# A two-block layer on one core: four products turned to tokens on partitions, seven accumulators in the first pass, and two paces of the scan

## The chip, the cores and the metric

One core of a Trainium2 chip runs the whole program. The metric is the time of one execution on the device in microseconds (us), smaller is better; the runs of before gave 2216.6, 2218.7 and 2218.76 us, median 2218.7 us.

## What is computed

Two blocks act one after the other on x, 256 tokens by 2048 features; the second (attention and a recurrent mix, then a gated feed-forward) is not touched. The first, cut to what matters:

```python
h = rmsnorm(x, norm_g)
proj = einsum('bld,dn->bln', h, w_in)
v, bg, cg, za, u, zb, ga, gb = split(proj, SPLITS)   # 2048 x4, 1024 x2, 2048 x2 columns
ya = bg * causal_depthwise_conv(cg * v, conv_w)
ya = einsum('blc,cd->bld', ya * silu(za), w_out_a)
yb = gelu(s5_scan(u, ...))                           # 64 groups, 64 complex states each
yb = yb * sigmoid(yb @ w_glu + b_glu)
yb = einsum('blc,cd->bld', yb * silu(zb), w_out_b)
m = sigmoid(ga) * ya + sigmoid(gb) * yb
return x + einsum('bld,de->ble', m, w_o)             # then rmsnorm with final_g
```

All of it is in 32-bit floats. To keep that precision on TensorE, each operand is split into a high part (rounded to fp32r) and a low part (the rest), and a product is the sum of high x high, low x high and high x low.

## The kernel before

**Weights.** All weights come in blocks of 128 x 1024 floats (512 KB), in the order in which the program wants them: `weights` makes the list from `W1` and `W2`, `sub` (line 241) hands out 128 columns of the present block. A block is loaded into `wf` by SyncE's queue, four ahead. ScalarE casts it to the high part `wh` (line 142 is every ScalarE operation), and VectorE subtracts to get the low part `wl` (line 132 is every two-operand operation on VectorE or GpSimd). Cast and split are recorded three blocks ahead of the use.

**Products.** `gemm` (line 255) makes 128 outputs for 256 tokens with the outputs on partitions: per 128 x 128 weight tile one matmul with `wh` stationary and the 512 columns of x's high and low part moving, and one with `wl` stationary and the 256 columns of the high part. This text calls the two a pair. The result lies in two halves of a PSUM bank, which are added when they are read: `take` (line 285) is a ScalarE copy, a VectorE add, and, where asked, a VectorE multiply with `R`, the reciprocal norm of each token. `v_in` (line 1392), in the second block, makes its product the other way around: x is stationary, 128 tokens at a time, and 512 weight columns move; three matmuls of 512 columns (high x high, high x low, low x high) per half of the tokens. Its result has tokens on partitions.

**Order of the work.** The program is written out in order for every engine; nothing is scheduled afterwards. `later` (line 156) starts a generator whose steps are recorded between the matmuls: each pair calls `tick` once, and a `yield n` lets n ticks pass (without a number, the task's default). `flush` records what is left at once. So a step's place among the matmuls is fixed, and each engine does its own list in order.

**First block.** `_block1` (line 792) loads and scales x (`X`), and runs `w_in`: a first pass over 12 of 16 rows of X with eight PSUM accumulators, one per tile of 128 columns of u, then the last four rows tile by tile (`u_out`). PSUM has eight banks, three named `acc` and five named `pb`. `squares` adds the squares of x on ScalarE and GpSimd, `first_norm` waits 96 ticks and has `rstd` (line 336) sum them with a matmul into `st`, and spread the result `R` with another into `al`. Then follow 16 rounds of v, cg, bg, za, each 16 pairs, which leave `Ya`. Then come w_out_a (to DRAM as `ya_out`), `w_in_g` (the columns of zb, ga, gb), w_glu, w_out_b with `merge_out`, and w_o with `x1_out`.

**The scan.** `s5` (line 621) runs as a task beside all this from the second row of X to the end of gb. `s5_prep` (line 421) makes its constants in steps of 8 ticks; `s5_base` (line 567) makes a table on GpSimd in steps of 1 to 3. Then come 32 steps of six yields of 8 ticks: two matmuls into `bu`, two VectorE products, two GpSimd sums, two VectorE scans (line 683), a GpSimd and a VectorE product, two GpSimd differences, and a table for the next step (ScalarE and GpSimd). Every fourth step sums its output with matmuls into `y` and starts `gelu`. `s5_stage` (line 554) brings the inputs by DMAs that GpSimd issues. At the end the rows of yb are split (`Yh`), which w_glu reads.

Of the kernel before, what the change touches and what calls it, by code (L numbers as in the profile page):

```python
# [10 lines left out]
F32 = mybir.dt.float32  # L11
F32R = mybir.dt.float32r
I32 = mybir.dt.int32
AF = mybir.ActivationFunctionType
# [72 lines left out]
class K:  # L87
# [74 lines left out]
    def _go(self, t):  # L162
        try:
            r = next(t[0])
            t[1] = t[3] if r is None else r
            return True
        except StopIteration:
            t[0] = None
            return False
# [136 lines left out]
    def hl(self, n, name="x"):  # L306

        c = [self.chunk(F32R, name) for _ in range((n + 3) // 4)]
        both = lambda k: self.flat(c[k // 4])[:, 512 * (k % 4):512 * (k % 4) + 512]
        return [(both(k)[:, 0:256], both(k)[:, 256:512], both(k)) for k in range(n)]  # L310

# [309 lines left out]
    def s5(self, U):  # L621

        nc, g = self.nc, self.nc.gpsimd
        for n in self.s5_prep():
            yield n or 8
        self.stg = self.flat(self.chunk(F32R, "stg")).rearrange("p (h i j t) -> p h i j t", h=2, i=2, j=2)
        stage = self.later(self.s5_stage(0), ev=False)
        cb = self.flat(self.cbd).rearrange("p (i k c) -> p i k c", i=2, k=32)
# [114 lines left out]
        yield  # L743
        self.tt(dst, z[:], sg[:], eng=self.nc.gpsimd)

    def ga_out(self, p, dst, ya):
        z, sg = self.tmp("z"), self.tmp("sg")
        yield from self.take(p, z[:], self.R[:])
        yield
        self.act(sg[:] if ya is not None else dst, z[:], AF.Sigmoid)  # L750
        if ya is not None:
            yield
            self.tt(dst, sg[:], ya[:], eng=self.nc.gpsimd)

    def glu_out(self, p, q, y, zb, dst):
        sg, t = self.tmp("sg"), self.tmp("ya")
        self.tt(t[:], y, zb, eng=self.nc.gpsimd)
# [8 lines left out]
        yield  # L766
        yield from self.hilo(t[:], dst)

    def merge_out(self, p, gb, ga, dst):
        t = self.tmp("ya")  # L770
        yield from self.take(p, t[:], gb)
        yield
        self.tt(t[:], t[:], ga, ALU.add, self.nc.gpsimd)
        yield
        yield from self.hilo(t[:], dst)

    def x1_out(self, p, n, x1, xin, dst):
        self.add(p, x1)
# [13 lines left out]
    def _block1(self):  # L792
        nc, g = self.nc, self.nc.gpsimd
        R, R2 = self.R, self.R2
        xin = [self.chunk(name="x") for _ in range(2)]
        X = self.hl(16, "X")

        def load(b):
            nc.sync.dma_start(out=xin[b // 4][:, 2 * (b % 4):2 * (b % 4) + 2], in_=self.i["x"][:, 2 * b:2 * b + 2])

        def scale(k):
            src = xin[k // 8][:, k % 8]
            g_ = self.vec("norm_g", k)
            self.act(X[k][0], src, scale=g_)
            self.stt(X[k][1], src, g_, X[k][0].bitcast(F32), ALU.mult, ALU.subtract)

        def squares():
            for k in range(16):
                sq = self.square(0, xin[k // 8][:, k % 8], first=k == 0)
                yield 2  # L810
                self.add_square(sq)
                yield 3
            self.squared = True

        for b in range(4):
# [12 lines left out]

        def first_norm():
            yield 96  # L830
            self.act(self.eps[:, 2:3], self.eps[:, 0:1], AF.Sqrt)
            yield 8
            yield from self.rstd(1, self.rt, R[:])
            self.tt(R2[:], R[:], R[:])

        self.setup2()
        norm = self.later(first_norm(), default=4)
        self.fg1 = self.const.tile([128, 16], F32, name="fg1")
        self.tt(self.fg1[:], self.vec("final_g"), self.vec("norm1_g"))
        U, uh = self.chunk(name="u"), [self.chunk(F32R, "uh") for _ in range(2)]  # L840
        self.cv = [self.const.tile([128, 258], F32, name=f"cv{i}") for i in range(2)]
        for c in self.cv:
            nc.vector.memset(c[:, 0:2], 0.0)
        ps = [self.pb("acc") if q in (0, 2, 4, 6, 7) else self.acc() for q in range(8)]
        self.s5u, self.s5b = ([self.dram.tile([128, 8, 256], F32, name=f"s5{n}{i}") for i in range(2)] for n in "ub")
        self.gelus, self.u_done, self.squared = 0, 0, False
        self.later(squares(), ev=False)
        for k in range(12):
            if k + 5 < 16:
                scale(k + 5)  # L850
            if k == 1:
                s5 = self.later(self.s5(U), ev=False, default=8)
            for p in ps:
                self.gemm(X[k:k + 1], p, k == 0, False)
        for q in range(8):
            p = self.gemm(X[12:16], ps[q], False, True)
            self.later(self.u_out(p, q, U[:, q], [c[:, q] for c in uh]))
        Ya = self.hl(16, "ya")
        for f in range(16):
            p = self.gemm(X)  # L860
            if f == 0:
                self.flush(norm)
            vs = self.tmp("vs", bufs=1)
# [10 lines left out]
        ya_out = self.dram.tile([128, 16, 256], F32, name="ya_out")  # L874
        for n in range(16):
            p = self.gemm(Ya)
            t = self.tmp("yo")
            self.take_now(p, t[:])
            nc.sync.dma_start(out=ya_out[:, n], in_=t[:])
        Ga, Zb = [self.chunk(name="ga") for _ in range(2)], self.chunk(name="zb")  # L880
        for q in range(8):
            p = self.gemm(X)
            self.later(self.silu_out(p, Zb[:, q]))
        for n in range(16):
            t = self.tmp("yo")
            nc.sync.dma_start(out=t[:], in_=ya_out[:, n])
            p = self.gemm(X)
            self.later(self.ga_out(p, Ga[n // 8][:, n % 8], t))
        Gb = [self.chunk(name="gb") for _ in range(2)]
        for n in range(16):  # L890
            p = self.gemm(X)
            self.later(self.ga_out(p, Gb[n // 8][:, n % 8], None))
# [12 lines left out]
        for n in range(16):  # L905
            p = self.gemm(Yg)
            self.later(self.merge_out(p, Gb[n // 8][:, n % 8], Ga[n // 8][:, n % 8], M[n]))
        xin = [self.chunk(name="x") for _ in range(2)]
        for k in range(0, 16, 8):
            nc.sync.dma_start(out=xin[k // 8][:], in_=self.i["x"][:, k:k + 8])  # L910
        self.x1 = self.dram.tile([128, 16, 256], F32, name="x1")
        self.flush()
        X2 = self.hl(16, "X")
        for n in range(16):
            p = self.gemm(M)
            self.later(self.x1_out(p, n, xin[n // 8][:, n % 8], xin, X2[n]))
            if n == 12:
                self.act(self.eps[:, 2:3], self.eps[:, 0:1], AF.Sqrt)
        self.flush()
        return X2  # L920

# [648 lines left out]


W2 = ("z_in", "v_in0", "v_in1", "qk_in", "v_in2", "w_out_at", "w_out_rw", "gate_up0", "down0", "gate_up1", "down1")
W1 = ("w_in", "w_out_a", "w_in_g", "w_glu", "w_out_b", "w_o")


def tiles(w, cols=128, kblk=None):
# [16 lines left out]
def layout(a):  # L1593
# [10 lines left out]
    u = r["w_in"][:16].reshape(8, 2, 128, 8, 128)  # L1604
    u = u.transpose(1, 3, 2, 0, 4).reshape(16, 128, 8, 128)
    r["w_in"][:12] = u[:12].reshape(12, 128, 1024)
    r["w_in"][12:16] = u[12:].reshape(4, 128, 4, 2, 128).transpose(2, 1, 3, 0, 4).reshape(4, 128, 1024)
    r["w_in_g"] = tiles(part(72, 40))
    for n in ("w_out_a", "w_glu", "w_out_b", "w_o"):
        r[n] = tiles(a[n][0])  # L1610
# [75 lines left out]
```

## Time and profile before

| | |
|---|---|
| median of three runs | 2218.7 us (2216.6 to 2218.76) |
| profiled execution | 2216.1 us, span of its instructions 2214.4 us |
| mean granted TensorE clock | 0.991 |
| first block | from 6.3 us (first matmul) to 944 us |

How to read the views: the page gives each engine's busy time and, in 40 slices of 55 us, its busy tenths. The table of waits says which engine stood idle before an instruction and what ended it. A row on a tile lists the instructions that read or write it, with shortest, median and longest duration and the first and last start. A row on a stretch gives each engine's busy time in it and the number of instructions. The timeline gives start, duration, engine, line, operation, and in brackets the idle time ahead of it and its releaser. Durations of matmuls are modelled ends; their starts are exact, so rates are read from starts.

### The profile page before, as it was taken

To read this page: it belongs to the slowest core of one execution; us is meant where nothing else is said; L and a number is where in the kernel's file an instruction comes from. 1 tells how busy PE (TensorE), PEld (TensorE's weight loads), DVE (VectorE), ACT (ScalarE), POOL (GpSimd) and SP (SyncE) were. 2 spreads that over 40 slices of the span, in tenths; PEclk is the share of its full clock that TensorE was granted. 3 is DMA by queue.
4 is the path that set the end of the run, shared out by engine and by line. 5 is a ranking of instruction groups with operands and counts; after the bars stand their busy time and mean duration, and the time that the engine had idled before them with its cause. 6 is when DMAs were issued, how large, how long until landed. Compare 5 with 4: busy or idle time off the path is not lost.

```text
span 2214.4 us, 37860 instructions
## 1 busy us (share of the span) xinstructions
PE 2151.8 (97%) x14500; PEld 1886.5 (85%) x14500; DVE 1655.3 (75%) x2396; ACT 1129.6 (51%) x1871; POOL 800.3 (36%) x930
## 2 busy tenths in 40 slices
PE   7899999999999999999989999999999999999997
PEld 6788888878888888899989888888888888888886
DVE  8889999987898678766896978976665555666554
ACT  5465555555555565544544544554444334444443
POOL 4768888866897012323330000421111001111111
PEclk9999999999999999999999999999999999999998
DMA  7586665667676657665646535566666666666653
GB/s 243 170 252 187 185 180 181 191 196 219 186 213 208 186 180 229 209 203 184 181 134 198 165 113 178 176 182 190 186 185 190 184 188 184 188 186 186 190 182 113
DMA packets 141842, 414.13 MB, mean 187 GB/s; under 512 B 27403, under 2 KB 46140, under 8 KB 140508
## 3 DMA queue, kind: packets, MB, share of 16 engines
q1 hardware_dynamic: 132540, 400.98, 59.3%
q0 software_dynamic: 8256, 8.40, 1.5%
q8 instruction: 114, 1.87, 0.3%
q10 hardware_dynamic: 864, 2.33, 0.3%
q14 instruction: 68, 0.56, 0.1%
HBM read 397.99 MB, written 15.75 MB: 187 GB/s over the span
## 4 chain that ended last, share of the span: by engine, by line
PE 75%; DVE 13%; DMA 4%; POOL 3%; issue 3%; ACT 1%; SPq 0%; DVEq 0%; ACTq 0%; POOLq 0%
PE acc L145 72%; DVE wl L132 5%; DMA wf<-z_in 2%; POOL s L132 1%; ACT wh L142 1%; PE y L145 1%; DMA wf<-w_in 1%; DVE gb L132 1%; DVE att L132 1%; DVE s L132 1%; DMA stg<-s5b 1%; DVE s L683 1%; DVE cv L132 0%; DVE ya L132 0%; POOL ab L132 0%
## 5 line engine op out<-in xcount | busy, mean ns | idle before, releaser
L145 PE MATMUL acc<-X,wh 128*128 128x512 f32 (+1 forms) x4576 | 1391.8, 366 | 6.3 <-ACT wh L142 6.3
L132 DVE TENSOR_TENSOR wl<-wf,wh 128x1024 fp32r<-128x1024 f32 (+1 forms) x711 | 937.8, 1322 | 306.3 <-ACT wh L142 302.1
L145 PE MATMUL acc<-X,wl 128*128 128x256 f32 x3888 | 1065.8, 283 | 14.6 <-DVE wl L132 14.5
L142 ACT ACTIVATE wh<-wf 128x1024 fp32r<-128x1024 f32 (+1 forms) x711 | 748.5, 1054 | 490.0 <-PE acc L145 339.3
L145 PEld LDWEIGHTS acc<-X,wh 128*128 128x128 f32 x4576 | 810.4, 190 | 140.9 <-ACT wh L142 6.3
L145 PEld LDWEIGHTS acc<-X,wl 128*128 128x128 f32 x3888 | 739.1, 190 | 42.1 <-DVE wl L132 22.8
L132 POOL TENSOR_TENSOR z<-z,R 128x256 f32<-128x256 f32 x44 | 58.9, 1338 | 523.4 <-ACT sg L142 523.4
L145 PE MATMUL acc<-s,wh 128*128 128x512 f32 (+1 forms) x726 | 246.8, 392 | 0.0
L132 POOL TENSOR_TENSOR s<-s 128x32 f32<-128x32 f32 (+4 forms) x272 | 223.7, 842 | 35.4 <-DVE s L132 19.1
L145 PE MATMUL acc<-s,wl 128*128 128x256 f32 x704 | 192.7, 281 | 0.0
L145 PEld LDWEIGHTS acc<-s,wh 128*128 128x128 f32 x726 | 133.0, 188 | 28.9
L132 POOL TENSOR_TENSOR sum<-sum,sq 128x256 f32<-128x256 f32 x74 | 71.4, 974 | 222.4 <-ACT sq L142 222.0
L145 PEld LDWEIGHTS acc<-s,wl 128*128 128x128 f32 x704 | 133.0, 189 | 3.2
L132 POOL TENSOR_TENSOR s<-s,s 128x256 f32<-128x256 f32 (+1 forms) x80 | 102.7, 1300 | 38.6 <-DVE s L132 24.4
L142 ACT ACTIVATE z<-acc 128x256 f32<-128x256 f32 x100 | 38.1, 381 | 117.2 <-PE acc L145 117.0
L145 PE MATMUL acc<-ya,wh 128*128 128x512 f32 x256 | 91.1, 403 | 0.1
L145 PE MATMUL acc<-m,wh 128*128 128x512 f32 x256 | 89.3, 398 | 0.0
L132 POOL TENSOR_TENSOR bv<-bv,gs 128x128 f32<-128x128 f32 x16 | 13.2, 832 | 205.4 <-DVE bv L139 205.4
L132 DVE TENSOR_TENSOR h<-acc,h 128x256 f32<-128x256 f32 x111 | 46.9, 422 | 43.0 <-PE acc L145 39.6
L142 ACT ACTIVATE s<-s,s 128x64 f32<-128x64 f32 (+2 forms) x192 | 69.4, 409 | 12.8 <-POOL s L132 11.6
L132 DVE TENSOR_TENSOR z<-acc,z 128x256 f32<-128x256 f32 x100 | 41.7, 417 | 45.2 <-ACT z L142 45.2
L145 PE MATMUL acc<-ya,wl 128*128 128x256 f32 x256 | 70.3, 284 | 4.0 <-ACT ya L142 3.1
(279 smaller groups left out, 2490.4 us busy)
## 6 DMA issues: line engine op xcount, KB each, us to landing
wf<-gate_up SPq DMA_DIRECT2D x176, 512.0 KB, 3.5
wf<-w_in SPq DMA_DIRECT2D x143, 512.0 KB, 4.4
wf<-down SPq DMA_DIRECT2D x88, 512.0 KB, 3.6
wf<-w_in_g SPq DMA_DIRECT2D x80, 512.0 KB, 3.6
wf<-z_in SPq DMA_DIRECT2D x54, 512.0 KB, 4.9
wf<-w_out_a SPq DMA_DIRECT2D x32, 512.0 KB, 4.3
wf<-w_o SPq DMA_DIRECT2D x32, 512.0 KB, 4.2
wf<-qk_in SPq DMA_DIRECT2D x32, 512.0 KB, 4.1
```

Source lines behind the costliest of these rows:

```text
L132: (eng or self.nc.vector).tensor_tensor(out=out, in0=a, in1=b, op=op)
L142: self.nc.scalar.activation(out=out, in_=a, func=f, **k)
L145: self.nc.tensor.matmul(out, l, r, start=start, stop=stop)
L683: nc.vector.tensor_tensor_scan(out=s[:, 256 * i:256 * i + 256], data0=r, data1=x[:, 256 * i:256 * i + 256], initial=0.0, op0=ALU.mult, op1 ...
```

## The change

1. **Tokens on partitions.** `by_token` replaces `gemm` for w_out_a, ga, gb and w_out_b, in the manner of `v_in`: for each 512 outputs two accumulators (one `acc`, one `pb`), one per half of the tokens, three matmuls of 512 columns each per row of x, and a tick for every 256 outputs. The four weight matrices are laid out in tiles of 512 columns for it. The results are read by one operation: w_out_a by a ScalarE copy, the gates by a ScalarE sigmoid whose scale is the token's reciprocal norm (`ga_out`), w_out_b by a VectorE multiply with the gate (`merge_out`). The sum of both branches is then turned back to features on partitions by TensorE transposes (`mt`), 32 in all, and split into `M`; the first w_o product starts on its first 12 rows before the last are made.
2. **Seven tiles of u.** The first pass has seven accumulators (three `acc`, four `pb`); the eighth tile is a product of 16 pairs behind the others. `first_norm` waits 62 ticks in place of 96, `squares` 4 per row in place of 5. The weights of u are laid out in the new order.
3. **Two paces.** A yield of the scan lasts 10 ticks up to the end of w_in (1152 pairs) and 7 afterwards, in place of 8; one of its setup 9 in place of 8.

```diff
     def _go(self, t):
         try:
             r = next(t[0])
-            t[1] = t[3] if r is None else r
+            t[1] = r if r is not None else t[3]() if callable(t[3]) else t[3]
...
     def s5(self, U):
         for n in self.s5_prep():
-            yield n or 8
+            yield n or 9
...
+    def by_token(self, xs, out):
+        n = len(xs)
+        for c in range(4):
+            ps = [self.acc(), self.pb("acc")]
+            for k in range(n):
+                wh, wl = self.sub(4)
+                xh, xl, _ = xs[k]
+                for t in range(2):
+                    ts_ = slice(128 * t, 128 * t + 128)
+                    self.mm(ps[t][:], xh[:, ts_], wh, k == 0, False)
+                    self.mm(ps[t][:], xh[:, ts_], wl, False, False)
+                    self.mm(ps[t][:], xl[:, ts_], wh, False, k == n - 1)
+                    if k == n - 1:
+                        out(c, t, ps[t])
+                    self.tick()
+                    self.tick()
+
+    def ga_out(self, p, t, dst, ya):
+        self.act(dst, p[:], AF.Sigmoid, scale=self.rt[:, t:t + 1])
+        if ya is not None:
+            yield 4
+            self.tt(dst, dst, ya[:], eng=self.nc.gpsimd)
+
+    def merge_out(self, p, c, t, ga, gb, M):
+        cs = slice(512 * c, 512 * c + 512)
+        self.tt(gb[t][:, cs], p[:], gb[t][:, cs])
+        yield 3
+        self.tt(ga[t][:, cs], ga[t][:, cs], gb[t][:, cs], ALU.add, self.nc.gpsimd)
+        if t == 0:
+            return
+        yield 6
+        for i in range(2):
+            n = 4 * c + 2 * i
+            q = self.pb("mt")
+            for j in range(4):
+                o = 128 * (n + j // 2)
+                self.nc.tensor.transpose(q[:, 128 * j:128 * j + 128], ga[j % 2][:, o:o + 128], self.ident[:])
+            v = M[n // 4][:, 512 * (n % 4):512 * (n % 4) + 1024].rearrange("p (k i t) -> p k i t", k=2, i=2)
+            yield from self.hilo(q[:].rearrange("p (k t) -> p k t", k=2), (v[:, 0], v[:, 1]))
...
                 self.add_square(sq)
-                yield 3
+                yield 2
...
         def first_norm():
-            yield 96
+            yield 62
...
-        ps = [self.pb("acc") if q in (0, 2, 4, 6, 7) else self.acc() for q in range(8)]
+        ps = [self.acc() if q in (1, 3, 5) else self.pb("acc") for q in range(7)]
...
-                s5 = self.later(self.s5(U), ev=False, default=8)
+                s5 = self.later(self.s5(U), ev=False, default=lambda: 10 if self.n_sub < 1152 else 7)
...
-            p = self.gemm(X[12:16], ps[q], False, True)
+            p = self.gemm(X[12:16], ps[q], False, True) if q < 7 else self.gemm(X, self.pb("acc"))
...
-        for n in range(16):
-            p = self.gemm(Ya)
-            t = self.tmp("yo")
-            self.take_now(p, t[:])
-            nc.sync.dma_start(out=ya_out[:, n], in_=t[:])
+        def wa_out(c, t, p):
+            y = self.tmp("yo", 512)
+            self.act(y[:], p[:])
+            nc.sync.dma_start(out=ya_out[:, t, 512 * c:512 * c + 512], in_=y[:])
+
+        self.by_token(Ya, wa_out)
...
-        for n in range(16):
-            p = self.gemm(Yg)
-            self.later(self.merge_out(p, Gb[n // 8][:, n % 8], Ga[n // 8][:, n % 8], M[n]))
+        mc = self.hl_chunks
+        self.by_token(Yg, lambda c, t, p: self.later(self.merge_out(p, c, t, Ga, Gb, mc)))
...
-            p = self.gemm(M)
+            if n == 0:
+                p = self.acc()
+                self.gemm(M[0:12], p, True, False)
+                self.flush()
+                X2 = self.hl(16, "X")
+                p = self.gemm(M[12:16], p, False, True)
+            else:
+                p = self.gemm(M)
```

Where instructions move, on TensorE. First, the sums of squares, matmul `st`, in the u stage (`acc` are the accumulators, X the rows of x). Before it stands behind the products of the second tile's last four rows:

```order
L145 MATMUL acc_167<-X_101,wl_501 128x256
L145 MATMUL acc_167<-X_101,wh_489 128x512
L145 MATMUL acc_167<-X_101,wl_501 128x256 x2
L145 MATMUL acc_167<-X_101,wh_489 128x512
L145 MATMUL st_604<-ones,sum_88 128x1 x2
L145 MATMUL acc_168<-X_101,wh_521 128x512
L145 MATMUL acc_168<-X_101,wl_531 128x256
```

Now it stands in the first pass, at the end of the tenth row:

```order
L145 MATMUL acc_171<-X_100,wl_374 128x256
L145 MATMUL acc_172<-X_100,wh_351 128x512
L145 MATMUL acc_172<-X_100,wl_374 128x256
L145 MATMUL st_476<-ones,sum_88 128x1 x2
L145 MATMUL acc_166<-X_100,wh_351 128x512
L145 MATMUL acc_166<-X_100,wl_374 128x256
```

It has moved from behind 104 pairs to behind 70, and no accumulator's bank has to be read before it. Second, the first rows of w_out_a; before, pairs of 512 and 256 columns into one accumulator:

```order
L145 MATMUL acc_4795<-ya_749,wh_4702 128x512
L145 MATMUL acc_4795<-ya_749,wl_4712 128x256
L145 MATMUL acc_4795<-ya_749,wh_4702 128x512
L145 MATMUL acc_4795<-ya_749,wl_4712 128x256
L145 MATMUL acc_4795<-ya_749,wh_4702 128x512
```

Now groups of three for each of two accumulators:

```order
L145 MATMUL acc_4657<-wh_4568,ya_756 128x512
L145 MATMUL acc_4657<-wl_4578,ya_756 128x512
L145 MATMUL acc_4657<-wh_4568,ya_756 128x512
L145 MATMUL acc_4658<-wh_4568,ya_756 128x512
L145 MATMUL acc_4658<-wl_4578,ya_756 128x512
L145 MATMUL acc_4658<-wh_4568,ya_756 128x512
```

All of w_out_a, ga, gb and w_out_b reads so. Third, a piece of the start of w_o, where only its own pairs stood; now the last transposes (`mt`, of the sums in `ga`) stand among them:

```order
L145 MATMUL acc_8129<-m_7768,wh_8059 128x512
L145 MATMUL acc_8129<-m_7768,wl_8074 128x256
L798 MATMUL mt_8151<-ident,ga_5461 128x128
L798 MATMUL mt_8151<-ident,ga_5462 128x128
L798 MATMUL mt_8151<-ident,ga_5461 128x128
L798 MATMUL mt_8151<-ident,ga_5462 128x128
L145 MATMUL acc_8129<-m_7768,wh_8059 128x512
```

Four more follow three pairs later, and the rows of `M` that they make are read from the 13th and the 15th pair on.

## Rows read from the trace of the kernel before

**Rows 1.** The page: span, and TensorE's and the other engines' busy time.
```profile
PE 2151.8 (97%) x14500; PEld 1886.5 (85%) x14500; DVE 1655.3 (75%) x2396; ACT 1129.6 (51%) x1871; POOL 800.3 (36%) x930
```
**Rows 2.** The page: busy tenths in 40 slices of VectorE and GpSimd.
```profile
DVE  8889999987898678766896978976665555666554
...
POOL 4768888866897012323330000421111001111111
```
**Rows 3.** Waits of TensorE, 0 to 112 us: total, times, longest.
```profile
PE acc L145 <- DVE wl L132: 8.4, 7, 2.9
...
PE st L145 <- DVE u L132: 3.3, 1, 3.3
```
**Rows 4.** Waits of TensorE, 112 to 455 us.
```profile
PE acc L145 <- DVE wl L132: 6.1, 10, 1.2
```
**Rows 5.** Waits of TensorE, 455 to 944 us.
```profile
PE acc L145 <- ACT ya L142: 3.1, 1, 3.1
PE acc L145 <- DVE wl L132: 0.9, 1, 0.9
```
**Rows 6.** Busy time in three stretches: length, PE, PEld, DVE, ACT, POOL, PEclk, DMA, GB/s.
```profile
53.40:56.80 3.40, 3.40 (x12) 2.81 (x12) 1.66 (x3) 0.47 (x2) 3.40 (x13) 0.51 0.94 274
90.90:97.70 6.80, 5.97 (x19) 5.10 (x20) 5.81 (x6) 1.80 (x2) 6.80 (x5) 0.50 0.36 85
466.40:469.80 3.40, 3.40 (x12) 2.84 (x11) 2.92 (x4) 3.37 (x8) 1.24 (x3) 0.50 0.30 73
```
**Rows 7.** Tile X on TensorE, 1146.1 to 1155.2 us (the v columns).
```profile
L145 PE MATMUL acc<-wl,X x14: 387/389/390, 1146.2 to 1155.1; 128*128 128x512 f32 x14
```
**Rows 8.** Tile m on TensorE (the w_o product).
```profile
L145 PE MATMUL acc<-m,wl x256: 277/281/285, 854.0 to 943.8; 128*128 128x256 f32 x128
```
**Rows 9.** Timeline of VectorE from 45 to 54 us.
```profile
49.84 2.40 DVE L132 TENSOR_TENSOR wl<-wf,wh 128x1024 fp32r<-128x1024 f32 x2
52.16 0.74 DVE L132 TENSOR_TENSOR u<-acc,u 128x256 f32<-128x256 f32 x2
```
**Rows 10.** Timeline of VectorE from 86 to 92 us.
```profile
87.32 2.36 DVE L132 TENSOR_TENSOR bd<-sm 64x512 f32<-64x512 f32 x2 [1.64 <-POOL sm L132]
89.71 1.97 DVE L132 TENSOR_TENSOR wl<-wf,wh 128x1024 fp32r<-128x1024 f32 x1
```
**Rows 11.** Busy time in four stretches, columns as in rows 6.
```profile
112.00:455.00 343.00, 335.75 (x1938) 286.70 (x1937) 312.21 (x377) 192.08 (x357) 273.85 (x304) 1.00 0.65 195
466.00:555.00 89.00, 89.00 (x510) 76.82 (x511) 68.57 (x75) 49.25 (x88) 58.51 (x78) 0.98 0.76 218
555.00:600.00 45.00, 45.00 (x269) 38.63 (x268) 39.55 (x44) 25.91 (x49) 36.22 (x42) 1.00 0.65 185
600.00:711.00 111.00, 111.00 (x646) 96.24 (x646) 102.16 (x110) 63.70 (x116) 94.67 (x99) 1.00 0.70 208
```
**Rows 12.** Groups of GpSimd, 466 to 555 us (first row) and 555 to 711 us.
```profile
L132 POOL TENSOR_TENSOR s<-s 128x512 f32<-128x512 f32 x3 | 3.9, 1294 | 2.4 <-DVE s L683 2.1
...
L132 POOL TENSOR_TENSOR zb<-z,sg 128x256 f32<-128x256 f32 x8 | 9.3, 1164 | 4.4 <-ACT sg L142 4.4
L132 POOL TENSOR_TENSOR s<-s,s 128x512 f32<-128x512 f32 x5 | 7.8, 1561 | 3.9 <-DVE s L683 3.9
```
**Rows 13.** Groups of VectorE, 455 to 711 us: count, busy us, mean ns, idle before.
```profile
L132 DVE TENSOR_TENSOR wl<-wf,wh 128x1024 fp32r<-128x1024 f32 x88 | 133.1, 1517 | 27.2 <-ACT wh L142 27.1
L683 DVE TENSOR_TENSOR_SCAN s<-s5r,s 128x256 f32<-128x256 f32 x30 | 25.0, 871 | 3.2 <-POOL s L132 3.2
L132 DVE TENSOR_TENSOR s<-bu,s 128x512 f32<-128x512 f32 x28 | 17.9, 678 | 0.0
L132 DVE TENSOR_TENSOR z<-z,R 128x256 f32<-128x256 f32 x27 | 15.6, 578 | 0.9
L132 DVE TENSOR_TENSOR z<-acc,z 128x256 f32<-128x256 f32 x27 | 10.9, 404 | 0.4 <-ACT z L142 0.4
```
**Rows 14.** Groups of TensorE over the whole span: transposes of the second block.
```profile
L1029 PE MATMUL tr<-ident,gb 128*128 128x128 f32 x32 | 4.9, 274 | 0.0
```

More of the change, by code (lines that the diff above doesn't have):

```diff
@@ L308, in hl @@
         c = [self.chunk(F32R, name) for _ in range((n + 3) // 4)]
+        self.hl_chunks = [self.flat(x) for x in c]
         both = lambda k: self.flat(c[k // 4])[:, 512 * (k % 4):512 * (k % 4) + 512]
@@ L744, in silu_out @@
         self.tt(dst, z[:], sg[:], eng=self.nc.gpsimd)
[L746 to L753, printed above, removed]
     def glu_out(self, p, q, y, zb, dst):
@@ L767, in glu_out @@
         yield from self.hilo(t[:], dst)
[L769 to L775, printed above, removed]
+    def by_token(self, xs, out):
[33 more added lines that the diff above has]
+                self.nc.tensor.transpose(q[:, 128 * j:128 * j + 128], ga[j % 2][:, o:o + 128], self.ident[:])
+            v = M[n // 4][:, 512 * (n % 4):512 * (n % 4) + 1024].rearrange("p (k i t) -> p i k t", k=2, i=2)
+            yield from self.hilo(q[:].rearrange("p (k t) -> p k t", k=2), (v[:, 0], v[:, 1]))
     def x1_out(self, p, n, x1, xin, dst):
@@ L873, in _block1 @@
         self.flush()
-        ya_out = self.dram.tile([128, 16, 256], F32, name="ya_out")
-        for n in range(16):
-            p = self.gemm(Ya)
-            t = self.tmp("yo")
-            self.take_now(p, t[:])
-            nc.sync.dma_start(out=ya_out[:, n], in_=t[:])
-        Ga, Zb = [self.chunk(name="ga") for _ in range(2)], self.chunk(name="zb")
+        ya_out = self.dram.tile([128, 2, 2048], F32, name="ya_out")
+        def wa_out(c, t, p):
[3 more added lines that the diff above has]
+        self.by_token(Ya, wa_out)
+        Ga, Zb = [self.flat(self.chunk(name="ga")) for _ in range(2)], self.chunk(name="zb")
         for q in range(8):
@@ L883, in _block1, with gate_a @@
             self.later(self.silu_out(p, Zb[:, q]))
-        for n in range(16):
[L885 to L892, printed above, removed]
+        def gate_a(c, t, p):
+            y = self.tmp("yo", 512)
+            nc.sync.dma_start(out=y[:], in_=ya_out[:, t, 512 * c:512 * c + 512])
+            self.later(self.ga_out(p, t, Ga[t][:, 512 * c:512 * c + 512], y))
+        self.by_token(X, gate_a)
+        Gb = [self.flat(self.chunk(name="gb")) for _ in range(2)]
+        self.by_token(X, lambda c, t, p: self.later(self.ga_out(p, t, Gb[t][:, 512 * c:512 * c + 512], None)))
         self.flush(s5)
@@ L904, in _block1 @@
         M = self.hl(16, "m")
-        for n in range(16):
-            p = self.gemm(Yg)
-            self.later(self.merge_out(p, Gb[n // 8][:, n % 8], Ga[n // 8][:, n % 8], M[n]))
+        mc = self.hl_chunks
+        self.by_token(Yg, lambda c, t, p: self.later(self.merge_out(p, c, t, Ga, Gb, mc)))
         xin = [self.chunk(name="x") for _ in range(2)]
@@ L911, in _block1 @@
         self.x1 = self.dram.tile([128, 16, 256], F32, name="x1")
-        self.flush()
-        X2 = self.hl(16, "X")
+        X2 = None
         for n in range(16):
-            p = self.gemm(M)
+            if n == 0:
[6 more added lines that the diff above has]
+                p = self.gemm(M)
             self.later(self.x1_out(p, n, xin[n // 8][:, n % 8], xin, X2[n]))
@@ L1572 @@
 W2 = ("z_in", "v_in0", "v_in1", "qk_in", "v_in2", "w_out_at", "w_out_rw", "gate_up0", "down0", "gate_up1", "down1")
-W1 = ("w_in", "w_out_a", "w_in_g", "w_glu", "w_out_b", "w_o")
+W1 = ("w_in", "w_out_a", "w_in_z", "w_in_ga", "w_in_gb", "w_glu", "w_out_b", "w_o")
 def tiles(w, cols=128, kblk=None):
@@ L1603, in layout @@
     r["w_in"] = tiles(np.concatenate(order, axis=1))
[L1604 to L1610, printed above, removed]
+    order = [(t, k) for k in range(12) for t in range(7)]
+    order += [(t, k) for t in range(7) for k in range(12, 16)] + [(7, k) for k in range(16)]
+    u = r["w_in"][:16].reshape(8, 2, 128, 8, 128).transpose(0, 1, 3, 2, 4).reshape(8, 16, 128, 128)
+    u = np.stack([u[t, k] for t, k in order]).reshape(16, 8, 128, 128)
+    r["w_in"][:16] = u.transpose(0, 2, 1, 3).reshape(16, 128, 1024)
+    r["w_in_z"], r["w_in_ga"], r["w_in_gb"] = tiles(part(72, 8)), tiles(part(80, 16), 512), tiles(part(96, 16), 512)
+    for n, m in (("w_out_a", 512), ("w_glu", 128), ("w_out_b", 512), ("w_o", 128)):
+        r[n] = tiles(a[n][0], m)
     st = lambda v: v.reshape(32, 2, 64).transpose(1, 2, 0).reshape(128, 32)
```

## Prediction

> **What bounds the kernel now.** I read the page first: TensorE is busy for 97% of the span, VectorE for 75% [rows 1]. The slices then say where the other engines are close to it: VectorE stands at eight and nine tenths until about 710 us, GpSimd at six to nine tenths over most of the same stretch [rows 2]. So there are two ways to gain: fewer TensorE nanoseconds for the same products, anywhere, and fewer waits of TensorE ahead of 470 us. The table of waits, asked in three stretches, lists the second. Up to 112 us seven waits for a split weight block (`wl`, made by VectorE) take 8.4 us and one wait of the matmul that sums the squares (`st`) 3.3 us [rows 3]; from 112 to 455 us ten more waits for `wl` take 6.1 us [rows 4]; and at the start of w_out_a one wait for the last `ya` takes 3.1 us [rows 5]. Three of these waits are followed by a stretch at half the granted clock, 1.2 instead of 2.4 GHz: two of 3.4 us and one of 6.8 us [rows 6]. From 470 us to the end of the first block TensorE hardly waits at all.
>
> **Products by token.** The four products move from 16 outputs of pairs (512 columns with the high half, 256 with the low) to tokens on partitions (three matmuls of 512 columns per token half). Per weight block of 1024 columns that is 16 matmuls before and 12 now, and 6144 columns both times. The kernel already has such a product: in the v columns of the second block the 14 matmuls with `wl`, one in each group of three, start from 1146.2 to 1155.1, so a group takes 8.9 / 13 = 0.685 us, 0.228 us for one of 512 columns [rows 7]. A pair of the w_o product takes (943.8 - 854.0) / 255 = 0.352 us [rows 8]. A block costs 8 x 0.352 = 2.82 us in pairs and 12 x 0.228 = 2.74 us by token. With 32 + 32 + 32 + 16 = 112 blocks, 0.08 us each: **-9.2 us** (bounds -8 and -10.5, from the rounding of the starts).
>
> **The start of w_out_a.** In the old form its 16th row of `ya` is wanted at the 16th pair, 15 x 0.352 = 5.3 us into the product; by token it is wanted only after 15 groups of two halves, 15 x 2 x 0.685 = 20.5 us. The wait of 3.1 us [rows 5] goes, and with it the half clock of 3.4 us behind it [rows 6], which costs half of itself: **-4.8 us**. What is late next there is a `wl` (0.9 us once before it); I leave that as it is.
>
> **Seven tiles of u.** All five banks of `pb` are taken by the first pass now, so `st` waits for the first u tile to be read. VectorE does that read only at 52.2 us, behind two splits [rows 9]. With seven tiles a bank is free, and `st` stands 34 pairs earlier. The 3.3 us and half of the 3.4 us at low clock go: **-5.0 us**. But the chain from `st` to `R` now runs while VectorE is at its fullest, with four ticks (one tick is one pair) between its links, 1.4 us; VectorE ran 3 us behind there [rows 3, 9]. The matmul that spreads `R` can wait for its diagonal: between 0 and 5 us, **+1.5** taken, since the sums, whose adds end earlier too, come well before.
>
> **Behind the u stage.** The `bd` writes of VectorE wait for GpSimd, then run at half their speed, 2.36 us for two, and a split stands behind them [rows 10]. That makes the longest of the seven waits, 2.9 us [rows 3], and the 6.8 us of half clock behind it, of which 6.0 us were work and so 3.0 us were lost [rows 6]: 5.9 us at this one place, and 8.6 us with half of the other six waits. The change spreads the setup (9 ticks for 8) and takes u's outputs away from it, but GpSimd's base table keeps its own pace. Bounds 0 and -8.6, the middle: **-4.5 us**.
>
> **The scan's two paces.** One step is six yields. Up to the end of w_in that is 60 ticks in place of 48, afterwards 42. VectorE is busy for 312 of 343 us from 112 to 455 us [rows 11], and the ten waits fall there late and in clusters, so its backlog is only just too large. A fifth fewer steps per time takes some 4% of its work and the GpSimd work that stretches it. I take the 6.1 us as gone: **-6.2 us** with the tails (bounds 0 and -7.2, what TensorE was not busy there [rows 11]).
>
> What pays for it: 19 steps are left after w_in where 15 were, and each gets 42 ticks, 14.4 to 14.8 us. From 466 to 555 us GpSimd does only the scan, 58.5 us of work in 89 us at 16.9 us a step [rows 11]: 11.1 us of work a step. In the z stage, 45 us, that is 3 x 11.1 and eight products of 1.16 us [rows 12], 43 us in 45; in gate a, 87 us, 6.1 x 11.1 and eight products of 1.3 to 1.56 us [rows 12], 79 us in 87. It was 36 of 45 and 95 of 111 [rows 11]. VectorE, on the other side, loses per output of gates and w_out_a a read of 0.40 us, and per gate output a multiply by R of 0.58 us [rows 13]: 48 x 0.40 + 32 x 0.58 = 38 us, which hides behind TensorE and is worth nothing there by itself, but keeps the splits early. A read that TensorE needs (`y`) stands three yields behind its last scan product, 7 us, so a GpSimd backlog under 5 us is covered. Bounds 0 and +10, from a backlog that is not covered: **+2 us**. The last rows of yb stand 12 ticks ahead of w_glu (91 before), 4 us that cover them.
>
> **The merge.** New on TensorE are 32 transposes; 32 of the same shape take 4.9 us of busy time, overlapping [rows 14]: **+4 us** (bounds 3.5 and 4.9). Each group of transposes stands 8 to 9 ticks, 3 us, behind the end of its accumulation and needs a product of 512 from PSUM (0.68 us [rows 13]) and a GpSimd sum (1.3 to 1.56 us [rows 12]), with up to one split of 1.5 us ahead of them: a wait of 0 to 0.6 us four times, and at the end the second half of the last `m` has only four ticks, 1.4 us, for its two copies, 0 to 2 us. **+2.5 us** (0 to 4.4). The w_out_b start gains from the late need of `yg` what it lost, under a microsecond; I set it at nothing, as I do the 8 larger transfers of `ya_out` in place of 16.
>
> **Sum.** -9.2 - 4.8 - 5.0 + 1.5 - 4.5 - 6.2 + 2 + 4 + 2.5 = -19.7 us. The profiled execution took 2216.1 us for a span of 2214.4 us, so 2196.4; the median of the runs is 2.6 us higher, 2218.7, and gives **2199 us**.
>
> **Rivals.**
> *All early waits go.* The `bd` waits vanish wholly, and neither `R`, the merge nor GpSimd makes a new one: another 4.1 + 1.5 + 2.5 + 2 us, about 2189. For it: VectorE was only just too slow. Against it: GpSimd's base table is untouched. 0.13.
> *Columns alone set the time.* If the 0.228 us in rows 7 is owed to something else in that place, 6144 columns cost the same either way: 2208. Against it: both stretches ran at the full granted clock and without a wait. 0.08. The Trainium skill speaks for this case: its page "TensorE: Matmul & The Clock Gate", section "Back-to-back issue gap", gives N/2.4 + 2.5 ns for a warm matmul, so four matmuls fewer would save an estimated 10 ns a block, 1.1 us over 112. By that rule the sum would be 2207; the trace does not agree, its pair of 0.352 us being longer than one and a half of 0.228.
> *VectorE stays late.* The waits of the scan stage and behind u remain, because they come from bursts and not from the mean load: 2199 + 6.2 + 4.5 = 2210. For it: the ten waits are of 1.2 us at most [rows 4], which a single burst can make. 0.14.
> *GpSimd falls behind in z and gate a.* 96% of its time is spoken for; a slowdown of a tenth (its 512-wide operations differ by a fifth from stage to stage [rows 12]) leaves it 4 us late, beyond the cover with a half-clock stretch of 1.7 us and a second wait: +8, 2207. 0.10.
> *Slower: the scan's own chain does not fit.* A step goes VectorE, GpSimd, VectorE, GpSimd, each needing the last: two products (1.4 us), two GpSimd sums (2.2), two scans (1.7 [rows 13]), one product (1.5), two differences (2.2), 9 us, and every hand-over can find a split of 1.5 us ahead of it. The point is 14.5 us a step; five such waits make 16.6. Then the steps keep their old 16.9 us, TensorE stands behind `bu` and `y`, and 19 x 2.4 us are lost: 2245. Against it: at 16.9 us TensorE waited for nothing in these stages. 0.05.
>
> **How the numbers follow.** The forecast has 0.50, with 2192 to 2206 as its own range from the bounds of the terms, which do not all fall on one side. From 2187 to 2211 the range takes in all rivals but the slow one and the low edge of the first, leaving out about 0.15. This kernel's measurement can tell about 0.2%, 4.4 us: faster means below 2214.3. All cases but the last lie below it; leaving 0.03 for the upper edge of "VectorE stays late", faster has 0.92, same 0.03, slower 0.05.
>
> **What would show it.** Right: in the four products three matmuls of 512 columns every 0.685 us; no wait of `st` above a microsecond; no wait for `ya`, and full clock at w_out_a; few waits for `wl` from 112 us to the end of w_in; GpSimd above nine tenths in z and gate a without a wait of TensorE. Wrong: a wait at the spreading of `R` above 5 us, TensorE idle behind `bu` or `y`, waits of the transposes (`mt`) above 4 us in sum, or groups of three at 0.70 us.

## The result, and the profile after

The changed kernel takes 2205.3 us (median of four runs, 2202.8 to 2206.6) beside 2218.7 us: a ratio of 0.994, interval 0.9923 to 0.9957. It is faster, by 13.4 us where 19.7 were forecast. The page of after: TensorE has 416 matmuls fewer (14500 before [rows 1]) and as large a share as before; the slices of VectorE and GpSimd are those of rows 2.

```profile
PE 2144.6 (97%) x14084; PEld 1867.1 (85%) x14084; DVE 1612.4 (73%) x2284; ACT 1116.7 (51%) x1791; POOL 804.1 (36%) x914
...
DVE  8889989988967666776896988966665556666553
...
POOL 3856777788879222323330001411111001111111
```

Where the time went is read by stage: the time from a stage's first main matmul to that of the next, by the starts in the two traces. I give the runs of the next section beside them. Each column is one profiled execution; before and after lie 9.7 us apart in it (spans of 2214.4 and 2204.7 us), 13.4 in the medians. How far one execution can be trusted is seen in w_in, where runs with the same code there differ by about 2 us (447.8 and 450.0; 434.1, 435.1 and, in merge_dve, 436.0).

| stage, us | before | after | early_load | tokens_only | tokens_early | paces_only | seven_only | best |
|---|---|---|---|---|---|---|---|---|
| w_in | 449.1 | 435.1 | 434.1 | 450.0 | 447.8 | 435.2 | 449.5 | 433.0 |
| w_out_a | 99.2 | 89.9 | 89.9 | 95.2 | 95.2 | 92.8 | 100.1 | 89.9 |
| z, ga, gb | 230.8 | 237.8 | 231.8 | 229.7 | 224.9 | 242.1 | 231.1 | 231.8 |
| w_glu | 22.6 | 22.6 | 22.6 | 22.6 | 22.6 | 22.6 | 22.6 | 22.6 |
| w_out_b | 45.8 | 50.1 | 50.1 | 50.1 | 50.1 | 45.8 | 45.7 | 46.3 |
| w_o | 90.3 | 93.0 | 93.1 | 93.1 | 93.1 | 90.3 | 90.3 | 91.5 |
| the rest | 1270.2 | 1269.6 | 1269.2 | 1270.3 | 1271.1 | 1270.9 | 1270.8 | 1268.8 |

After gains 14.0 us in w_in and 9.3 in w_out_a, and gives 7.0 back in z, ga and gb, 4.3 in w_out_b and 2.7 in w_o. The third row is the surprise: 64 of its 80 blocks became cheaper, and yet the stage got longer.

The waits of TensorE in after, up to 112 us (two rows, beside a wait for the first cast, ahead of the first matmul; they answer to rows 3) and from 455 to 944 us (four rows; rows 5). From 112 to 455 us the table is empty, where rows 4 had ten waits. The columns are total, times and longest.

```profile
PE acc L145 <- DVE wl L132: 7.7, 4, 5.1
...
PE al L145 <- DVE dg L136: 3.2, 1, 3.2
...
PE mt L798 <- POOL ga L132: 4.4, 4, 1.3
PE acc L145 <- DVE wl L132: 3.6, 4, 1.9
PE y L145 <- POOL s L132: 1.0, 1, 1.0
PE acc L145 <- ACT wh L142: 0.9, 1, 0.9
```

So `st` waits no more, but `al` does, 3.2 us where `st` had waited 3.3; the wait for `ya` is gone; and in z to gb, where before had none at all, there are waits now. Busy time of after by stretch, columns as in rows 6: the four stretches at half clock in the first block, two of 3.4 us in the u stage (before had one, at 53.4 us [rows 6]), 6.8 us at the place of `bd`, 3.4 us in gate a; then w_in from 112 us (rows 11), w_out_a, and about z, gate a and gate b (by its own first and last group gate a runs from 578.4 to 679.6 us).

```profile
30.10:33.50 3.40, 3.40 (x12) 2.89 (x11) 3.40 (x6) 1.39 (x3) 2.64 (x3) 0.50 0.38 147
47.10:50.50 3.40, 2.83 (x10) 2.58 (x11) 2.50 (x9) 0.33 (x2) 0.00 (x0) 0.50 0.50 153
94.90:101.70 6.80, 3.60 (x12) 3.12 (x13) 6.73 (x6) 1.36 (x2) 6.72 (x5) 0.50 0.25 77
647.90:651.30 3.40, 3.40 (x10) 2.62 (x9) 3.40 (x3) 3.37 (x8) 2.68 (x3) 0.50 0.58 176
...
112.00:441.60 329.60, 329.60 (x1913) 285.37 (x1913) 294.78 (x362) 190.45 (x332) 229.07 (x249) 1.00 0.67 204
441.70:531.50 89.80, 89.80 (x413) 73.80 (x412) 75.92 (x71) 52.25 (x87) 76.87 (x90) 1.00 0.72 222
531.60:576.60 45.00, 45.00 (x269) 38.66 (x268) 37.57 (x41) 26.13 (x51) 40.44 (x48) 1.00 0.62 188
576.70:672.00 95.30, 89.61 (x407) 70.16 (x406) 69.58 (x64) 47.62 (x81) 76.84 (x92) 0.98 0.62 193
672.00:769.20 97.20, 96.99 (x441) 79.00 (x440) 70.73 (x66) 51.18 (x74) 55.69 (x56) 1.00 0.65 205
```

From 112 us to the end of w_in TensorE is busy without a gap, and GpSimd has 229 us of work where it had 274 [rows 11]. Nearly all of TensorE's idle time between 532 and 769 us lies in gate a, 5.7 of 95.3 us. The product itself is as fast as hoped: tile X from 735 to 765 us, in gate b, one row of 45 groups:

```profile
L145 PE MATMUL acc<-wl,X x45: 389/389/389, 735.0 to 764.9; 128*128 128x512 f32 x45
```

(764.9 - 735.0) / 44 = 0.680 us a group of three, 0.685 in rows 7.

What stands in the way of gate a is seen by going back from TensorE's first wait there, at 616 us, engine by engine: VectorE (first row) had no high part to split, since ScalarE (second) stood before a step of the scan's table, since GpSimd (third) stood before its product with `yo`, the row of `ya_out` that is loaded back, since that load (last, SyncE's queue) was issued at 604.6 us. These are single rows of four timelines of after, and GpSimd's wait in sum from 560 to 700 us.

```profile
617.30 2.84 DVE L132 TENSOR_TENSOR wl<-wf,wh 128x1024 fp32r<-128x1024 f32 x2 [7.65 <-ACT wh L142]
...
614.60 0.91 ACT L142 ACTIVATE s<-s,s 128x256 f32<-128x256 f32 x2 [7.98 <-POOL s L132]
...
610.88 1.29 POOL L132 TENSOR_TENSOR ga<-ga,yo 128x512 f32<-128x512 f32 x1 [5.39 <-DMA yo<-ya_out]
...
604.60 0.90 SPq L914 DMA_DIRECT2D yo<-ya_out  x2
...
POOL ga L132 <- DMA yo<-ya_out: 10.9, 4, 5.4
```

Before, the load of `ya_out` was issued ahead of each gate product; the change issues it in `gate_a`, behind the product's last matmul, four ticks (1.4 us) ahead of its use, while the transfer takes 5.3 us from issue to landing (median in after) and is itself queued behind weight loads.

### The profile page after: what moved, and what is told of

It reads as the page before. It is cut to its first block, busy times and chain, and to the rows that moved or that the text cites. A ratio compares the mean times of both kernels' runs of the same rounds, so it can differ in the third digit from the quotient of the medians.

```text
span 2204.7 us, 36780 instructions
## 1 busy us (share of the span) xinstructions
PE 2144.6 (97%) x14084; PEld 1867.1 (85%) x14084; DVE 1612.4 (73%) x2284; ACT 1116.7 (51%) x1791; POOL 804.1 (36%) x914
## 4 chain that ended last, share of the span: by engine, by line
PE 78%; DVE 9%; POOL 5%; DMA 3%; issue 2%; ACT 1%; SPq 0%; DVEq 0%; ACTq 0%; POOLq 0%
PE acc L145 75%; DVE wl L132 3%; DMA wf<-z_in 2%; POOL s L132 1%; POOL ga L132 1%; ACT wh L142 1%; DVE gb L132 1%; POOL sm L132 1%; POOL ab L132 1%; PE y L145 1%; DVE att L132 1%; DMA yo<-ya_out 0%; DMA wf<-qk_in 0%; POOL base L132 0%; DVE scr L139 0%
## 5 line engine op out<-in xcount | busy, mean ns | idle before, releaser
L145 PE MATMUL acc<-X,wh 128*128 128x512 f32 (+1 forms) x4064 | 1212.5, 363 | 6.6 <-ACT wh L142 6.6
L145 PE MATMUL acc<-X,wl 128*128 128x256 f32 x3376 | 925.7, 282 | 8.4 <-DVE wl L132 8.4
L145 PEld LDWEIGHTS acc<-X,wh 128*128 128x128 f32 x4064 | 716.6, 190 | 121.4 <-ACT wh L142 6.6
L145 PEld LDWEIGHTS acc<-X,wl 128*128 128x128 f32 x3376 | 642.3, 190 | 27.4 <-DVE wl L132 10.8
L145 PE MATMUL acc<-wh,X 128*128 128x512 f32 (+1 forms) x704 | 210.0, 376 | 0.9 <-ACT wh L142 0.9
L145 PEld LDWEIGHTS acc<-wh,X 128*128 128x128 f32 x704 | 130.1, 190 | 26.1 <-ACT wh L142 1.3
L145 PE MATMUL acc<-wl,X 128*128 128x512 f32 (+1 forms) x352 | 132.1, 375 | 3.6 <-DVE wl L132 3.6
L132 POOL TENSOR_TENSOR s<-s,s 128x256 f32<-128x256 f32 (+1 forms) x80 | 112.6, 1424 | 31.0 <-DVE s L684 15.4
L145 PEld LDWEIGHTS acc<-wl,X 128*128 128x128 f32 x352 | 66.9, 190 | 17.2 <-DVE wl L132 6.4
L145 PE MATMUL acc<-wh,ya 128*128 128x512 f32 x256 | 80.3, 390 | 0.0
```

The source lines that it names most:

```text
L132: (eng or self.nc.vector).tensor_tensor(out=out, in0=a, in1=b, op=op)
L145: self.nc.tensor.matmul(out, l, r, start=start, stop=stop)
```

## The experiments

Theory L: this late load is what gate a loses. Rival G: GpSimd is simply full at 42 ticks a step. For the first stage, theory V: VectorE's own work sets the time, and a wait taken away comes back as another. Before, measured with each batch, had medians of 2216.2, 2216.4 and 2216.3 us.

**early_load: the load in the middle of the product.**

```diff
+                if mid is not None and k == n // 2:
+                    mid(c)
...
+        def load_a(c):
+            for t in range(2):
+                ys[t] = self.tmp("yo", 512)
+                nc.sync.dma_start(out=ys[t][:], in_=ya_out[:, t, 512 * c:512 * c + 512])
...
-        self.by_token(X, gate_a)
+        self.by_token(X, gate_a, load_a)
```

> The changed kernel with one thing moved: the two loads of ya_out for a group of 512 gate columns are issued in the middle of that group's product instead of behind it. Theory L (late load): in gate a GpSimd stands in front of its product with yo until the load lands (10.9 us in four waits), the scan behind it slips, ScalarE's table steps hold up the casts, and TensorE loses about 8 us. L expects GpSimd's wait for yo to go, gate a without a wait of TensorE above 1 us, and 2195 to 2199 us. Rival G (GpSimd is simply full at 42 ticks a step): the waits of TensorE in gate a stay in sum, with other releasers, and the time is 2203 to 2206 us.

Measured: 2199.5 us, ratio 0.9928 (0.9913 to 0.9943). z, ga and gb take 231.8 us for 237.8. GpSimd no longer waits for `yo`; what TensorE waits for there are four splits, 2.1 us in sum, 0.8 at most. L holds, with 6 us in place of the 8 I gave it, and the time is 0.5 us above its range. The whole times alone would not show it, for the intervals of after and early_load overlap; the price is read from the stage.

```profile
576.70:672.00 95.30, 93.23 (x431) 73.94 (x430) 80.37 (x71) 51.65 (x88) 87.29 (x100) 1.00 0.68 214
...
PE acc L145 <- DVE wl L132: 2.1, 4, 0.8
```

In the same 95.3 us GpSimd is now busy for 87.3 us, 92%, and TensorE stands idle for 2.1.

**tokens_only: the four products alone**, in the late form of the change, with eight tiles and 8 ticks.

> The kernel before with the four products by token alone (the load of ya_out behind the product, as in the change), with eight tiles of u and the pace of 8 ticks. Columns -9, start of w_out_a -5, merge +7. L expects that GpSimd still waits for yo in gate a, but with more room behind it (16.9 us a step), so that TensorE loses 2 to 6 us there: 2212 to 2218 us. G expects no wait in gate a at this pace: 2209 to 2212 us.

Measured: 2218.1 us, ratio 1.0006 (0.9997 to 1.0016): no difference, and 0.1 us above what L said. The stages show why: w_out_a gains 4.0 us and z to gb 1.1, and the merge costs 7.1 in w_out_b and w_o. GpSimd waits for `yo` even longer, 21.2 us in four waits:

```profile
POOL ga L132 <- DMA yo<-ya_out: 21.2, 4, 6.3
```

At the start of w_out_a there is no wait for `ya` any more, but other waits and a stretch at half clock have taken its place (waits of TensorE from 455 to 552 us, and the busy time of the stretch, columns as in rows 6):

```profile
PE acc L145 <- DVE wl L132: 1.7, 2, 1.0
PE acc L145 <- ACT wh L142: 1.1, 1, 1.1
...
468.40:471.80 3.40, 3.25 (x8) 2.58 (x9) 2.91 (x5) 3.03 (x5) 1.23 (x4) 0.50 0.61 182
```

**tokens_early: the same with the load in the middle.**

> tokens_only (eight tiles, 8 ticks) with the loads of ya_out in the middle of the product. L: GpSimd's 21 us of waiting for yo go; z, ga and gb take 226 to 228 us for 229.7, w_in stays at 450, the whole 2214 to 2216 us beside 2218.1. G, that the pace of 7 costs what is left over in gate a of early_load (231.8 us, of which about 2 us are the four more scan steps): 226 to 228 us too, but then 2 us of it are the pace's; if 229 us or more, the pace costs nothing and the load neither.

Measured: 2211.2 us, ratio 0.9975 (0.9966 to 0.9984). z, ga and gb take 224.9 us, 4.8 less than in tokens_only, less than either theory gave. Here the whole times show it too: the ten runs of each kernel do not overlap (2210.5 to 2212.9 us, 2215.1 to 2219.0). So the late load costs 4.8 us at the old pace and 6.0 at the new one, and the pace costs 8.1 us with the late load (237.8 - 229.7) and 6.9 with the early one (231.8 - 224.9): both theories hold a part. Of the 6.9 us, 2.3 are the matmuls of the scan steps that moved here (24 `bu` for 16, 64 `y` for 48, by start distances), and 4.6 are main matmuls that take longer (224.6 us for 220.0). By start distances 3.2 of the 4.6 lie at early_load's four waits, which show 2.1 us of idle time, and 0.9 at shorter hold-ups.

**paces_only: the two paces alone on the kernel before.**

```diff
-            t[1] = t[3] if r is None else r
+            t[1] = r if r is not None else t[3]() if callable(t[3]) else t[3]
...
-            yield n or 8
+            yield n or 9
...
-                s5 = self.later(self.s5(U), ev=False, default=8)
+                s5 = self.later(self.s5(U), ev=False, default=lambda: 10 if self.n_sub < 1152 else 7)
```

> The kernel before with the two paces of the scan alone. The waits for split blocks between 112 and 455 us go, as in the changed kernel (-11 us). L expects the gates, where before loads ya_out ahead of each product, to stay free of waits: 2206 to 2209 us. G expects GpSimd to fall behind with z and ga at 14.8 us a step, and TensorE to wait 5 us or more between 540 and 720 us: 2212 to 2218 us.

Measured: 2208.0 us, ratio 0.9964 (0.9951 to 0.9977). w_in falls to 435.2 us, all of what after gains there, and no wait is left from 112 to 455 us; w_out_a, still in pairs, has none either and gains 6.4 us. In z, ga and gb 11.3 us come back, though `ya_out` is loaded early here: TensorE waits for splits, 6.5 us in seven waits.

```profile
112.00:441.00 329.00, 329.00 (x1912) 284.91 (x1910) 290.29 (x363) 190.37 (x332) 228.66 (x249) 1.00 0.68 204
...
PE acc L145 <- DVE wl L132: 6.5, 7, 1.5
```

The total lies in L's range, but by luck: L had the gates free of waits, and G was right about them; w_in and w_out_a gained more than L gave them. With the products in pairs VectorE still has its reads and its multiplies with R there [rows 13], and the faster scan costs 11.3 us; by token it costs 6.9. That fits a worth of the work taken off VectorE, which I had set at nothing, but no run takes that work away alone.

**seven_only: seven tiles, the earlier norm and squares alone.**

> The kernel before with seven tiles of u, the earlier norm and the faster squares alone. Theory V (VectorE sets the time of this stage): the wait of st goes and the matmul that spreads R (al) waits instead, the long wait behind bd stays, 2216 to 2220 us. Rival P (the prediction's terms -5.0 +1.5 and part of -4.5): 2211 to 2215 us, with al waiting 2 us or less.

Measured: 2217.7 us, ratio 1.0007 (0.9998 to 1.0017); w_in 449.5 us for 449.1. V's time and its wait came. `al` waits 4.2 us in place of 3.3 for `st`, and the splits 9.0 us in place of 8.4 [rows 3]:

```profile
PE acc L145 <- DVE wl L132: 9.0, 5, 3.1
...
PE al L145 <- DVE dg L136: 4.2, 1, 4.2
```

**norm_links: early_load with eight ticks between the links of the norm.**

```diff
-        norm = self.later(first_norm(), default=4)
+        norm = self.later(first_norm(), default=8)
```

> early_load with eight ticks instead of four between the links of the first norm's chain. The wait of al (3.3 us) goes in every theory. Theory V (VectorE sets the time up to about 70 us): TensorE then waits for a split instead, the w_in stage keeps its 434 us within 1.5 us, and the run is 2198 to 2200 us. Rival P (the wait of al is a loss of its own): 3 to 5 us less, 2195 to 2197 us.

Measured: 2198.5 us, ratio 0.9921 (0.9905 to 0.9937), w_in 435.0 us for 434.1. The wait of `al` halves, where both theories had it gone, and the splits take over what it lost: 9.8 us in seven waits where early_load has 8.3 in four. The time is V's.

```profile
PE acc L145 <- DVE wl L132: 9.8, 7, 3.4
...
PE al L145 <- DVE dg L136: 1.6, 1, 1.6
```

**merge_dve: early_load with one of the two merge sums on VectorE.**

```diff
-        self.tt(ga[t][:, cs], ga[t][:, cs], gb[t][:, cs], ALU.add, self.nc.gpsimd)
+        self.tt(ga[t][:, cs], ga[t][:, cs], gb[t][:, cs], ALU.add, self.nc.vector if t else self.nc.gpsimd)
```

> early_load with the second of the two sums of each merge on VectorE in place of GpSimd. Theory S: the transposes wait 4.4 us in four waits because both sums stand one behind the other on GpSimd, 1.75 us each; with one of 0.7 us on VectorE beside it they are ready 1.8 us earlier and the waits go: w_out_b 46 to 47 us for 50.1, and 4 us less in all than early_load (2199.5), 2195 to 2196. Rival D: VectorE's splits stand in front of the sum, the waits stay above 3 us, no change (2198 to 2200).

Measured: 2194.7 us, ratio 0.9901 (0.9885 to 0.9918). No wait is left from 780 to 944 us, w_out_b takes 46.3 us for 50.1 and w_o 91.5 for 93.1. What it removed, in GpSimd's timeline of early_load (the transposes come when both sums are done, 3.5 us after the first could start):

```profile
809.17 3.49 POOL L132 TENSOR_TENSOR ga<-ga,gb 128x512 f32<-128x512 f32 x2 [9.56 <-DVE gb L132]
```

**prep_dve: early_load with the setup's products ahead of `bd` on VectorE.**

```diff
-        self.tt(w1, x, a1, eng=g)
+        self.tt(w1, x, a1)
...
-            self.tt(u2, p2, bc(ni), eng=nc.gpsimd)
+            self.tt(u2, p2, bc(ni))
```

(and the seven other small sums and products beside the first.)

> early_load with the eight small sums and products behind the base table's steps and the two products u2 of the scan's setup on VectorE in place of GpSimd. Theory B: the long wait for a split near 90 us (5.4 us, and 6.8 us at half clock behind it) comes from VectorE standing at bd, 4.2 us, for GpSimd, which has the base table in front of u2; with that wait gone the w_in stage loses 5 to 8 us and the run is 2192 to 2195 us. Rival V: VectorE's own work sets the time of the stage, and 3.4 us more of it give the gain back: 2197 to 2200 us.

Measured: 2198.8 us, ratio 0.9923 (0.9901 to 0.9945); w_in 431.8 us for 434.1. In after (first row) VectorE stands 4.2 us before `bd` for GpSimd; with the products on VectorE that wait and the 6.8 us of half clock behind it are gone, but three waits for splits remain between 70 and 112 us (second row), where after had 5.5 us in three.

```profile
93.06 2.99 DVE L132 TENSOR_TENSOR bd<-sm 64x512 f32<-64x512 f32 x2 [4.18 <-POOL sm L132]
...
PE acc L145 <- DVE wl L132: 4.5, 3, 2.1
```

The wait is as B said, the time is V's: 2.3 us in w_in, not 5 to 8, and that is hardly more than runs with the same code differ by. The run's own time does not tell it from early_load.

**best: the edits of early_load, merge_dve and prep_dve together**, and **best_shift: best with a setup that starts slower.**

> early_load with the edits of merge_dve and prep_dve together. They act in different stages, so their gains should add: w_in 432 us, w_out_b 46.3, w_o 91.5, and 2191 to 2194 us. If they do not add: 2195 to 2199.

Measured: 2192.5 us, ratio 0.9892 (0.9876 to 0.9908), the fastest here, in the range named for gains that add: w_out_b and w_o take 46.3 and 91.5 us as in merge_dve, w_in 433.0 for the 432 expected. What prep_dve's edit adds to merge_dve (2194.7 us) is not clear of noise; the intervals overlap. The edit of best_shift:

```diff
-            yield n or 9
+            yield n or (13 if self.n_sub < 88 else 6)
```

> best with the scan's setup in steps of 13 ticks during the first 88 pairs and 6 afterwards, so that VectorE has about a third less of it in the first 45 us and the end of the setup stands 11 ticks earlier. Theory V (VectorE's work sets the time up to 70 us): the waits for a split near 26 and 35 us and that of al get shorter, together by 2 us or more, while the waits behind u may grow; w_in 429 to 432 us. Rival: the early waits come from the weights' loads, which compete with those of x; they stay within 1 us and w_in is 432 us or more.

Measured: 2195.8 us, ratio 0.9911 (0.9892 to 0.993); w_in takes 433.0 us in both. The waits before 70 us fall by 1.1 us; those from 70 to 140 us rise from 3.6 (first row, best) to 6.1 us (second, best_shift). V had named 2 us or more and 429 to 432 us for w_in, and neither came. What came is a shift: at the 256th main matmul best_shift is 4.2 us ahead of best, at the 500th 0.6 us behind. Work of VectorE that is moved inside this stage moves the wait with it. The rival, the loads, has not been tested by itself. That best_shift is 3.3 us slower lies outside w_in: in the two traces it loses 1.7 us between the start of z and w_out_b and 2.0 in the second block, for reasons that I did not trace.

```profile
PE acc L145 <- DVE wl L132: 3.6, 3, 3.1
...
PE acc L145 <- DVE wl L132: 6.1, 3, 3.6
```

## Why the prediction was right in sum and wrong in its parts

The time lies in the range, 6.3 us above the forecast. That the sum came so near is luck: the three terms of the u stage, -8.0 us together, gave nothing (w_in takes 435.1 us in after and 435.2 in paces_only), and the gates cost about 13 us where 2 were forecast, while the pace gave twice its term in w_in.

- **Columns, -9.2: right, and a little small.** A pair takes 0.352 us [rows 8], a group 0.680: per block 0.096 us, -10.8 over 112, just outside the bounds. The rival "columns alone" is out: with as many columns the main matmuls of w_out_b take 44.2 us in after for 45.8 in before, by start distances. In a group 512 columns take 0.227 us, in a pair 0.235; why the pair's take longer is not shown. The Trainium skill, page "TensorE: Matmul & The Clock Gate", section "Back-to-back issue gap", gives N/2.4 + 2.5 ns for an isolated warm matmul, 216 ns at 512 columns; the trace does not agree, its matmuls in long runs starting 227 ns apart, and the measurement decides.
- **The start of w_out_a, -4.8: the size near, the cause mostly another.** The stage gains 9.3 us, of which the columns are 3.1, so 6.2 lie at its start. The prediction put them down to the late need of `ya`. tokens_only has that late need at the old pace and gains 4.0 in all, so 0.9 at the start: the wait for `ya` goes, and waits for a cast and for splits, with 3.4 us at half clock, take its place. paces_only has the early need, no wait there at all, and gains 6.4. The slower scan in w_in removed this wait.
- **Seven tiles, -5.0 and +1.5: wrong.** The step that failed is "With seven tiles a bank is free", from which 5.0 us were to go, with `al` priced at 1.5 us apart from it. seven_only shows 0: the wait moved whole from `st` (3.3 us) to `al` (4.2). VectorE is busy for 58.8 of the 64 us from 6 to 70 us there, 55.7 in before, and two stretches of 3.4 us at half clock lie in them where before has one.
- **Behind u, -4.5: mostly wrong.** after still waits 5.1 us once and has 6.8 us at half clock behind it. prep_dve takes away the cause that I had named, and w_in falls by 2.3 us: other splits wait in its place.
- **The scan's pace in w_in, -6.2: the mechanism right, the size half.** paces_only and after gain 14 us, 2.0 of it scan matmuls that moved on (8 `bu` and 16 `y` fewer), 12 against my bound of 7.2. I had counted the idle time of the table. By start distances, what main matmuls take above their medians from 112 us to the end of w_in is 12.5 us in before and 0.9 in after. At the wait of 256 us in before (three rows of TensorE's timeline) the second matmul starts 1.56 us behind the first, for a usual 0.235, and the third 0.22 behind the second, for a usual 0.117: 1.4 us lost, of which the table has 1.16.

```profile
256.55 0.39 PE L145 MATMUL acc<-X,wh 128*128 128x512 f32 x1
258.11 0.39 PE L145 MATMUL acc<-X,wl 128*128 128x256 f32 x1 [1.16 <-DVE wl L132]
258.33 0.40 PE L145 MATMUL acc<-X,wh 128*128 128x512 f32 x1
```

- **The gates, +2: wrong, by the step that failed worst.** "I set it at nothing, as I do the 8 larger transfers of `ya_out`": I compared their number and size, not their place in the order. The load had moved from ahead of a product of 5.6 us to behind one. early_load prices it at 6.0 us. The rival "GpSimd falls behind" had the right engine and a price of the right size (+8), but 6.0 us of the cost came by the late load, not by GpSimd's own work. The pace's own cost here, 6.9 us, was outside my +2 and inside its bounds; the two together, 12.9 us, lie outside them.
- **The merge, +4 and +2.5: a little small in sum, and wrongly shared.** By start distances the transposes cost 8.1 us in after (5.9 in w_out_b, 2.2 in w_o), and 2.8 in best, where they do not wait. So 5.3 us are the waits, 4.4 of them idle time, just above the 4 that the prediction had named as a sign of being wrong. The sums take 1.75 us each with VectorE at work beside them, not 1.3 to 1.56; merge_dve moves one and no wait is left.
- **The slower rival** did not come: from 455 to 944 us TensorE waited for `y` 1.0 us in all, and 0.2 ahead of a `bu`.

What stays open: why splits come late in z to gb at the faster pace once the load is early, and whether GpSimd, busy for 92%, is the cause; no run slows or relieves it there by itself. And whether the u stage can be cut at all without taking work off VectorE there; no run tried that.

## What to carry to other kernels

When a part of a program that is ordered by hand is rewritten, list for every transfer what stood between its issue and its use before and what stands there now: a load that slid behind its product cost 6.0 us here, more than half of the 10.8 us that the products by token save in columns. Where one engine is busy throughout a stage, do not count a wait of another on it as a loss that can be taken out by itself: seven_only, norm_links and best_shift each shortened one wait on VectorE in the u stage, others took its place, and none has a time that shows a gain. And a slower pace in the full stage with a faster one in the emptier is worth more once the second has been emptied: 8 us alone (2216.2 - 2208.0), 12 us together with the products by token (2211.2 - 2199.5, with the seven tiles that gave nothing).

## What was not expected of the hardware

A group of three matmuls of 512 columns runs at 0.227 us each, with x stationary and weights moving; in a pair the 512 columns take 0.235 us and the 256 columns 0.117 (medians of start distances in after). What makes the difference is not shown. And two GpSimd sums of 512 take 3.49 us back to back while VectorE is at its splits, 1.75 us each, while a GpSimd operation of the same shape took 1.29 us in w_out_a of before [rows 12].
